# A two-layer hybrid trunk on one core: attention masks ahead of the scores, and one operand of each seven-product block summed by a second load

## The chip, the cores and the metric

The kernel runs on one core of one Trainium2 chip. The metric is device time in microseconds (us) of one execution. Engines are named as in the profile: PE does matrix products, PEld its weight loads, DVE is the vector engine, ACT the scalar engine, POOL the GpSimd engine, SP issues loads.

## What is computed

Two layers; in each, x passes through three sub-layers, every one between two RMSNorms and added back to x:

```
for l in range(DEPTH):                       # DEPTH 2, x is (1, 256, 1024) float32
    f = _swiglu(_rmsnorm(h, ff1_norm_pre[l]), ff1_w_gate[l], ff1_w_up[l], ff1_w_down[l])
    h = h + 0.5 * _rmsnorm(f, ff1_norm_post[l])
    m = _hybrid_mixer(_rmsnorm(h, mix_norm_pre[l]), w_in[l], ..., w_out[l])
    h = h + _rmsnorm(m, mix_norm_post[l])
    f = _swiglu(_rmsnorm(h, ff2_norm_pre[l]), ff2_w_gate[l], ff2_w_up[l], ff2_w_down[l])
    h = h + 0.5 * _rmsnorm(f, ff2_norm_post[l])

def _swiglu(h, wg, wu, wd):                  # 1024 -> 2816 -> 1024
    return (jax.nn.silu(h @ wg) * (h @ wu)) @ wd
```

The mixer puts three head groups side by side: a chunked state-space scan, a pooling group, and causal attention with four heads of 64 dimensions over the 256 tokens. Weights and results are float32.

## The kernel before

**Weights and precision.** Nearly all the work is weight matrices against 256 tokens. A weight comes in units of 128 x 2048 float32 (1 MB), loaded by SP (`load`, L77) into one of four `raw` buffers. Each unit, or a sum or difference of units, is a *job*: ACT writes `hi`, a copy rounded for the matrix engine (L102), DVE writes `lo = raw - hi` (L103), each in two pieces of 1024 columns. A job that is a sum first has DVE add two raw buffers (L101). A product of two split operands takes three passes: hi by hi, hi by lo, lo by hi. Up to five split jobs are held ahead of their use (`pump`, `get`, `done`).

**An FFN** has 2816 inner features in 11 blocks of 256. Blocks 0 and 1 are done token half by token half (`mm_half`, L317). Blocks 4, 7 and 10 are plain pairs of gate and up (`mm_feat`, L298). Blocks 2, 5 and 8, each with the one behind it, form a *quad*: a seven-product scheme in Strassen's manner (`ffn_quad`, with `product`, L428). The four quarters of a quad's weights are called g1, u1, g2 and u2, and its jobs are g1, u2, g2 and four sums: T1 = g1 + u1, T2 = T1 + u2, T3 = T2 - g1 (which is u1 + u2), T4 = T2 + g2. The left operands, S1 to S4 and parts X of the normalised tokens, are made at the start of each FFN (L281 to L287). Down projections (`mm_rows`, L334) of earlier blocks lie between the products of a quad. There are 3 quads in an FFN, 4 FFNs, so 12 quads.

In `plan_ffn` (L360 to L377) T1, T2 and T4 are built one upon the other in u1's raw buffer, T3 in g1's; g1's buffer is given back after T3, u1's after T4.

**Attention scores** (L676 to L686) are taken per row half: the two heads of a pair lie on rows 0 to 63 and 64 to 127. For each half and each pair a 128 x 128 block of scores (L683), its mask (a product of two bf16 constants that adds a large negative number, L684), a 128 x 256 block (L685) and a mask on its right half (L686) go one after another.

**Order.** The code is written once, and a scheduler puts each engine's instructions in an order of its own by their dependences; an engine then executes its own list strictly in that order, and waits where an operand isn't there. So a late operand holds up all that stands behind it on its engine.

Of the kernel before, what the change touches and what calls it, by code (L numbers as in the profile page):

```python
# [13 lines left out]
AF = mybir.ActivationFunctionType  # L14
ALU = mybir.AluOpType
AX = mybir.AxisListType

P = 128
# [29 lines left out]
class Weights:  # L48
# [9 lines left out]
        self.units.append((src, cols))  # L58
        return len(self.units) - 1

    def job(self, unit, sum_of=None, free=(), pieces=2):


        self.jobs.append((unit, sum_of, free, pieces))
        return len(self.jobs) - 1

    def plan(self, src, cols=UNIT, pieces=2):
# [18 lines left out]
    def split_next(self, only=None):  # L86

        i, nc = self.split, self.nc
        u, sum_of, free, pieces = self.jobs[i]
        cols, raw = self.units[u][1], self.raw[u]  # L90
        if i not in self.parts:
            self.parts[i] = [self.splitp.tile([P, KD * QDT], F32R, tag=x, name=f"{x}{i}") for x in ("hi", "lo")]
        hi, lo = self.parts[i]
        step = cols // pieces
        for c in range(0, cols, step):
            if only and c // step not in only:
                continue
            s = slice(c, c + step)
            if sum_of:
                x, op, y = sum_of  # L100
                nc.vector.tensor_tensor(raw[:, s], self.raw[x][:, s], self.raw[y][:, s], op=op)  # L101
            nc.scalar.activation(hi[:, s], raw[:, s], AF.Copy)  # L102
            nc.vector.tensor_tensor(lo[:, s], raw[:, s], hi[:, s].bitcast(F32), op=ALU.subtract)  # L103
        if only and pieces - 1 not in only:
            return
        for v in free:
            del self.raw[v]
            self.live -= 1
        self.split += 1
        self.held += 1  # L110
# [25 lines left out]
def hybrid_trunk_kernel(ctx: ExitStack, tc: tile.TileContext, a, out: bass.AP):  # L136
    nc = tc.nc
# [9 lines left out]
    def buf(dtype=F32, n=512, tag="t"):  # L147
        return tmp.tile([P, n], dtype, tag=tag, name=f"{tag}{next(ids)}", bufs={"t": 22, "n": 8}[tag])
# [4 lines left out]
    def bank(tag="wk"):  # L153
        return psum.tile([P, 512], F32, tag=tag, name=f"{tag}{next(ids)}")
# [4 lines left out]
    W = Weights(nc, rawp, splitp)  # L159
# [178 lines left out]
    def plan_ffn(l, n):  # L338


        p = {}

        def down(i):
            p["d", i] = W.plan(a[f"ff{n}_d"][l, i])

        def pair(i):
            for k in "gu":
                p[k, i] = W.plan(a[f"ff{n}_{k}"][l, PAIRS.index(i)])

        for i in range(2):  # L350
            for k in range(2):
                p["f", i, k] = W.plan(a[f"ff{n}_f"][l, 2 * i + k], pieces=4)
        before = list(FIRST)
        for i in range(2, NU):
            if i in PAIRS:
                pair(i)
                for b in before:
                    down(b)
                before = [i]
            elif i in QUADS:  # L360
                src = a[f"ff{n}_q"][l, QUADS.index(i)]
                g1, u1, u2 = (W.unit(src[k]) for k in (0, 1, 3))
                p["T1", i] = W.job(u1, (g1, ALU.add, u1))
                p["g1", i] = W.job(g1)
                p["T2", i] = W.job(u1, (u1, ALU.add, u2))
                p["T3", i] = W.job(g1, (u1, ALU.subtract, g1), free=(g1,))
                late = i == QUADS[-1]
                if not late:
                    down(before[0])
                g2 = W.unit(src[2])  # L370
                p["g2", i] = W.job(g2)
                for b in before[1:]:
                    down(b)
                p["T4", i] = W.job(u1, (u1, ALU.add, g2), free=(u1, g2))
                p["u2", i] = W.job(u2, free=(u2,))
                if late:
                    down(before[0])  # L377
                before = [i, i + 1]
        for b in before:
            down(b)  # L380
        return p
# [40 lines left out]
    def product(ps, left, job, first):  # L422

        hi, lo = (w[:, :UNIT].rearrange("p (k n) -> p k n", k=4) for w in W.get(job))
        parts = [(k, i) for i in range(3) for k in range(4)]
        for n, (k, i) in enumerate(parts):
            x, w = ((left[0], hi), (left[0], lo), (left[1], hi))[i]
            nc.tensor.matmul(ps, x[:, k, :], w[:, k, :], start=first and n == 0, stop=n == len(parts) - 1,  # L428
                             skip_group_check=not first)
        W.done(job)  # L430

    def ffn_quad(i, p, left, turn, downs):


        late = i == QUADS[-1]
        turn(0)
        pc = bank()
        product(pc, left["S1"], p["T1", i], True)
        h1 = buf()
        nc.scalar.activation(h1, pc, AF.Copy)  # L440
        pa = bank()
        product(pa, left["X11"], p["g1", i], True)
        w2 = buf()
        nc.scalar.activation(w2, pa, AF.Copy)
        turn(1)
        W.pump()
        pb = bank()
        product(pb, left["S2"], p["T2", i], True)
        nc.vector.tensor_tensor(w2, pb, w2, op=ALU.add)
        nc.vector.tensor_tensor(pc, pc, w2, op=ALU.subtract)  # L450
        W.pump()
        pd = bank()
        product(pd, left["S3"], p["T3", i], True)
        nc.vector.tensor_tensor(pd, pd, w2, op=ALU.add)
        nc.vector.tensor_tensor(h1, h1, pd, op=ALU.subtract)
        W.pump()
        if not late:
            downs[0]()
        product(pa, left["X12"], p["g2", i], False)
        h0 = buf()  # L460
        nc.scalar.activation(h0, pa, AF.Silu)
        W.pump()
        for f in downs[1:]:
            f()
        product(pd, left["X22"], p["T4", i], False)
        nc.scalar.activation(w2, pd, AF.Silu)
        nc.vector.tensor_tensor(h1, h1, w2, op=ALU.mult)
        W.pump()
        product(pc, left["S4"], p["u2", i], False)
        nc.vector.tensor_tensor(h0, pc, h0, op=ALU.mult)  # L470
        W.pump()
        if late:
            downs[0]()
        return [h0, h1]
# [74 lines left out]
    def mixer(l, p, turned, next_left, before_next):  # L549
# [125 lines left out]

        s0, s1 = banks2(), banks2()  # L676
        for j in range(2):
            r = slice(j * 64, (j + 1) * 64)
            for pr in range(2):
                q_ = qT[r, pr * 256 : (pr + 1) * 256]  # L680
                k_ = kT[r, pr * 256 : (pr + 1) * 256]
                o0, o1 = s0[j][:, pr * P : (pr + 1) * P], s1[j][:, pr * 256 : (pr + 1) * 256]
                nc.tensor.matmul(o0, q_[:, :P], k_[:, :P], start=True, stop=False)  # L683
                nc.tensor.matmul(o0, ident_b, neg_b, start=False, stop=True)  # L684
                nc.tensor.matmul(o1, q_[:, P:], k_, start=True, stop=False)  # L685
                nc.tensor.matmul(o1[:, P:], ident_b, neg_b, start=False, stop=True)  # L686

        def softmax(ps, n):

# [383 lines left out]
```

## Time and profile before

| | |
|---|---|
| runs | 963.24, 967.30, 967.02 us; median 967.02 |
| span of the profiled execution, the one time that it gives | 964.0 us |
| ACT busy | 583.2 us |
| L102, hi | 440 pieces, 399.6 us of ACT |
| L103, lo | 440 pieces, 466.4 us of DVE |
| read from memory | 176.07 MB |

The page gives the busy time of each engine, then groups of instructions: line, engine, operation, output and inputs, count, busy time and mean time of one, and how long the engine sat idle before them and for whom. A timeline row gives the start of an instruction or a run of like ones, its time, engine, line, tiles, count, and in square brackets the idle time before it with what ended it. A row of the view by stretches gives the time, the busy time and count of PE, PEld, DVE, ACT and POOL, the granted clock of the matrix engine (1.00 is full), the share of the DMA engines, and GB/s.

### The profile page before, as it was taken

What the parts mean: (1) busy time and instruction counts of PE and PEld (TensorE: products, weight loads), DVE (VectorE), ACT (ScalarE), POOL (GpSimd) and SP (SyncE); (2) the same over time, 40 slices, a digit from 0 to 9 for tenths busy, and PEclk for the clock granted to TensorE, in tenths of its full rate; (3) what the DMA queues carried; (4) which work ended last, traced back from release to release, by engine and by line L of the source; (5) the groups of instructions that cost most, each with busy time, mean ns of one, the idle gap of its engine ahead of it and who ended that gap; (6) DMA issues with size and microseconds to landing.
All of it is one profiled execution on the core that took longest, in us unless ns stands there. A gap on an engine that the chain in (4) does not pass through costs nothing.

```text
span 964.0 us, 13044 instructions
## 1 busy us (share of the span) xinstructions
PE 942.5 (98%) x5066; PEld 802.9 (83%) x5066; DVE 816.2 (85%) x1091; ACT 583.2 (61%) x923; POOL 21.8 (2%) x35
## 2 busy tenths in 40 slices
PE   7899999999999999999999999999999999999997
PEld 4689898888988779888977888888888877889896
DVE  6998899688787989889698989996878798989982
ACT  6655557477646565657466656666675565656651
POOL 0000000010001000000000000000000100000000
PEclk9989999998999999999999999999999999999999
DMA  8474456665243255455742737294733242827251
GB/s 327 151 266 171 177 216 241 242 209 184 89 159 119 90 201 237 169 225 215 265 174 85 276 112 294 88 343 161 270 121 131 88 154 88 330 99 301 85 190 44
DMA packets 26274, 177.96 MB, mean 185 GB/s; under 512 B 2914, under 2 KB 3170, under 8 KB 5732
## 3 DMA queue, kind: packets, MB, share of 16 engines
q1 hardware_dynamic: 26212, 177.13, 49.5%
q8 instruction: 40, 0.66, 0.3%
q14 instruction: 22, 0.18, 0.1%
HBM read 176.07 MB, written 1.05 MB: 184 GB/s over the span
## 4 chain that ended last, share of the span: by engine, by line
PE 74%; DVE 12%; ACT 8%; issue 3%; DMA 2%; POOL 1%; DVEq 0%; POOLq 0%; SPq 0%; ACTq 0%
PE acc L334 24%; PE wk L428 20%; PE wk L298 20%; DVE lo L103 5%; ACT hi L102 5%; PE wk L317 5%; DVE raw L101 2%; ACT n L223 2%; POOL s L217 1%; PE wk L403 1%; DVE n L207 1%; DMA raw<-in_ff_q 1%; DVE xT L207 1%; PE wk L863 1%; DVE n L249 1%
## 5 line engine op out<-in xcount | busy, mean ns | idle before, releaser
L102 ACT ACTIVATE hi<-raw 128x1024 fp32r<-128x1024 f32 (+2 forms) x440 | 399.6, 959 | 173.6 <-DVE raw L101 62.5
L103 DVE TENSOR_TENSOR lo<-raw,hi 128x1024 fp32r<-128x1024 f32 (+2 forms) x440 | 466.4, 1100 | 18.7 <-ACT hi L102 17.9
L334 PE MATMUL acc<-hi,t 128*128 128x512 f32 x832 | 221.9, 396 | 6.8 <-ACT hi L102 6.6
L334 PEld LDWEIGHTS acc<-hi,t 128*128 128x128 f32 x832 | 154.6, 189 | 42.1 <-ACT hi L102 9.1
L298 PE MATMUL wk<-xT,hi 128*128 128x256 f32 x1088 | 147.6, 288 | 0.0
L298 PEld LDWEIGHTS wk<-xT,hi 128*128 128x128 f32 x1088 | 140.1, 196 | 1.7
L334 PE MATMUL acc<-lo,t 128*128 128x512 f32 x416 | 116.0, 394 | 0.0
L101 DVE TENSOR_TENSOR raw<-raw,raw 128x1024 f32<-128x1024 f32 x96 | 113.8, 1216 | 2.0 <-DMA raw<-in_ff_q 2.0
L317 PE MATMUL wk<-hi,xT 128*128 128x512 f32 x384 | 101.3, 396 | 3.9 <-ACT xT L206 1.8
L428 PE MATMUL wk<-hi,n 128*128 128x512 f32 x384 | 101.8, 392 | 0.0
L334 PEld LDWEIGHTS acc<-lo,t 128*128 128x128 f32 x416 | 79.0, 190 | 16.9 <-DVE lo L103 0.2
L317 PEld LDWEIGHTS wk<-hi,xT 128*128 128x128 f32 x384 | 71.0, 188 | 21.7 <-ACT hi L102 3.1
L428 PEld LDWEIGHTS wk<-hi,n 128*128 128x128 f32 x384 | 71.6, 188 | 15.6 <-DVE wk L450 1.1
L298 PE MATMUL wk<-xT,lo 128*128 128x256 f32 x544 | 77.6, 285 | 0.0
L428 PE MATMUL wk<-hi,xT 128*128 128x512 f32 x288 | 77.2, 390 | 0.1
L298 PEld LDWEIGHTS wk<-xT,lo 128*128 128x128 f32 x544 | 71.1, 194 | 0.0
L428 PEld LDWEIGHTS wk<-hi,xT 128*128 128x128 f32 x288 | 53.6, 188 | 11.8 <-issue 0.5
L206 ACT ACTIVATE t<-wk 128x256 fp32r<-128x256 f32 x72 | 26.8, 377 | 55.4 <-PE wk L403 30.6
L317 PE MATMUL wk<-lo,xT 128*128 128x512 f32 x192 | 52.5, 393 | 1.1 <-DVE lo L103 1.0
L428 PE MATMUL wk<-lo,n 128*128 128x512 f32 x192 | 51.4, 390 | 0.0
L231 DVE TENSOR_TENSOR n<-acc,gains 128x512 f32<-128x512 f32 x24 | 16.5, 688 | 35.9 <-ACT n L223 35.9
L317 PEld LDWEIGHTS wk<-lo,xT 128*128 128x128 f32 x192 | 35.9, 188 | 10.0 <-DVE lo L103 2.3
(175 smaller groups left out, 764.6 us busy)
## 6 DMA issues: line engine op xcount, KB each, us to landing
raw<-in_ff_q SPq DMA_DIRECT2D x48, 1024.0 KB, 6.9
raw<-in_ff_d SPq DMA_DIRECT2D x44, 1024.0 KB, 6.5
raw<-in_ff_f SPq DMA_DIRECT2D x16, 1024.0 KB, 6.2
raw<-in_ff_g SPq DMA_DIRECT2D x12, 1024.0 KB, 5.8
raw<-in_ff_u SPq DMA_DIRECT2D x12, 1024.0 KB, 5.1
raw<-in_w_in SPq DMA_DIRECT2D x10, 1024.0 KB, 5.0
raw<-in_w_kvz SPq DMA_DIRECT2D x8, 1024.0 KB, 7.2
raw<-in_w_out SPq DMA_DIRECT2D x8, 1024.0 KB, 5.4
```

The source lines that it names most:

```text
L101: nc.vector.tensor_tensor(raw[:, s], self.raw[x][:, s], self.raw[y][:, s], op=op)
L102: nc.scalar.activation(hi[:, s], raw[:, s], AF.Copy)
L103: nc.vector.tensor_tensor(lo[:, s], raw[:, s], hi[:, s].bitcast(F32), op=ALU.subtract)
L206: split_into.last = nc.scalar.activation(hi, src_f32, AF.Copy)
L207: nc.vector.tensor_tensor(lo, src_f32, hi.bitcast(F32), op=ALU.subtract)
L217: nc.gpsimd.tensor_tensor(r, v, halfexp, op=ALU.pow)
L223: nc.scalar.activation(junk, x, AF.Square, scale=1.0 / (gain * math.sqrt(n)), accum_out=ssq)
L231: nc.vector.tensor_tensor(fg[i], f[i], gains[:, 1, i * 512 : (i + 1) * 512], op=ALU.mult)
L298: nc.tensor.matmul(ps, w[:, k, s], y[:, k, :], start=i == 0 and k == 0, stop=i == 2 and k == KD - 1)
L317: m = nc.tensor.matmul(ps, y[:, k, :], w[:, k, :], start=h == 0 and n == 0, stop=h == 1 and n == len(parts) - 1)
L334: nc.tensor.matmul(acc[b], x[:, j, s], w[:, j, b * 512 : (b + 1) * 512], start=first and j == 0 and i == 0, stop=last and j == 1 and i == 2)
L428: nc.tensor.matmul(ps, x[:, k, :], w[:, k, :], start=first and n == 0, stop=n == len(parts) - 1, skip_group_check=not first)
```

## The change

Two edits.

1. **Scores.** The eight mask products of a layer are done first, and the score products are then accumulated on top of them, with the row half as the innermost loop, so that neighbouring products lie on different row halves.
2. **Quads.** g1 is split first. T1, T2 and T4 are then built one upon the other in g1's raw buffer. As soon as T1's last add is done, POOL issues a second load of u2's 1 MB that adds to u1's raw buffer in place. T3 is then a plain job on that buffer, with no add on DVE, and u1's buffer is given back after T3. In `ffn_quad` g1's product moves ahead of T1's.

```
-    def job(self, unit, sum_of=None, free=(), pieces=2):
-        self.jobs.append((unit, sum_of, free, pieces))
+    def job(self, unit, sum_of=None, free=(), pieces=2, add=None):
+        self.jobs.append((unit, sum_of, free, pieces, add))
...
             if sum_of:
                 x, op, y = sum_of
                 nc.vector.tensor_tensor(raw[:, s], self.raw[x][:, s], self.raw[y][:, s], op=op)
+                if add and c + step == cols:
+                    nc.gpsimd.dma_start(self.raw[add[0]][:, :cols], add[1], accum_op=ALU.add)
...
-                p["T1", i] = W.job(u1, (g1, ALU.add, u1))
                 p["g1", i] = W.job(g1)
-                p["T2", i] = W.job(u1, (u1, ALU.add, u2))
-                p["T3", i] = W.job(g1, (u1, ALU.subtract, g1), free=(g1,))
+                p["T1", i] = W.job(g1, (g1, ALU.add, u1), add=(u1, src[3]))
+                p["T2", i] = W.job(g1, (g1, ALU.add, u2))
+                p["T3", i] = W.job(u1, free=(u1,))
...
-                p["T4", i] = W.job(u1, (u1, ALU.add, g2), free=(u1, g2))
+                p["T4", i] = W.job(g1, (g1, ALU.add, g2), free=(g1, g2))
...
         turn(0)
+        pa = bank()
+        product(pa, left["X11"], p["g1", i], True)
+        w2 = buf()
+        nc.scalar.activation(w2, pa, AF.Copy)
         pc = bank()
         product(pc, left["S1"], p["T1", i], True)
         h1 = buf()
         nc.scalar.activation(h1, pc, AF.Copy)
-        pa = bank()
-        product(pa, left["X11"], p["g1", i], True)
-        w2 = buf()
-        nc.scalar.activation(w2, pa, AF.Copy)
...
         for j in range(2):
-            r = slice(j * 64, (j + 1) * 64)
-            for pr in range(2):
-                q_ = qT[r, pr * 256 : (pr + 1) * 256]
-                k_ = kT[r, pr * 256 : (pr + 1) * 256]
-                o0, o1 = s0[j][:, pr * P : (pr + 1) * P], s1[j][:, pr * 256 : (pr + 1) * 256]
-                nc.tensor.matmul(o0, q_[:, :P], k_[:, :P], start=True, stop=False)
-                nc.tensor.matmul(o0, ident_b, neg_b, start=False, stop=True)
-                nc.tensor.matmul(o1, q_[:, P:], k_, start=True, stop=False)
-                nc.tensor.matmul(o1[:, P:], ident_b, neg_b, start=False, stop=True)
+            for ps, n, at in ((s0[j], P, 0), (s1[j], 2 * P, P)):
+                for pr in range(2):
+                    nc.tensor.matmul(ps[:, pr * n + at : pr * n + at + P], ident_b, neg_b, start=pr == 0, stop=False,
+                                     skip_group_check=True)
+        for pr in range(2):
+            for s, n, q0 in ((s0, P, 0), (s1, 2 * P, P)):
+                for j in range(2):
+                    r = slice(j * 64, (j + 1) * 64)
+                    nc.tensor.matmul(s[j][:, pr * n : (pr + 1) * n], qT[r, pr * 256 + q0 : pr * 256 + q0 + P],
+                                     kT[r, pr * 256 : pr * 256 + n], start=False, stop=True, skip_group_check=True)
```

The lines behind the new ones move down by two or three, so L102 and L103 become L104 and L105.

**ACT at the first quad of FFN2, layer 0.** In the rows before, raw_2878 is u1's buffer (T2 here), raw_2624 is g1's (T3 here) and raw_2902 the first down projection's.

```order
L102 ACTIVATE hi_3063<-raw_2878 128x1024
L206 ACTIVATE n_2994<-t_2981 128x512
L206 ACTIVATE n_2999<-t_2818 128x512
L206 ACTIVATE t_3089<-wk_3093 128x2x128
L102 ACTIVATE hi_3071<-raw_2624 128x1024
L102 ACTIVATE hi_3081<-raw_2902 128x1024
L102 ACTIVATE hi_3071<-raw_2624 128x1024
L102 ACTIVATE hi_3081<-raw_2902 128x1024
```

In the rows of the change, at the same place, raw_2621 is g1's buffer (T2 here), raw_2875 is u1's (T3, filled up by the accumulating load) and raw_2899 the first down projection's.

```order
L208 ACTIVATE n_2989<-t_2976 128x512
L208 ACTIVATE n_2994<-t_2815 128x512
L104 ACTIVATE hi_3061<-raw_2621 128x1024
L104 ACTIVATE hi_3069<-raw_2875 128x1024
L104 ACTIVATE hi_3061<-raw_2621 128x1024
L104 ACTIVATE hi_3069<-raw_2875 128x1024
L104 ACTIVATE hi_3077<-raw_2899 128x1024 x2
```

T3's halves were taken in turn with the down projection's; now they are taken in turn with T2's, and the down projection's stand behind both.

**DVE at the same place.** Before, with lo_3064 of T2, lo_3072 of T3 and lo_3082 of the first down projection:

```order
L103 TENSOR_TENSOR lo_3064<-raw_2878,hi_3063 128x1024
L101 TENSOR_TENSOR raw_2624<-raw_2878,raw_2624 128x1024 x2
L207 TENSOR_TENSOR t_3090<-wk_3093,t_3089 128x2x128
L103 TENSOR_TENSOR lo_3072<-raw_2624,hi_3071 128x1024
L103 TENSOR_TENSOR lo_3082<-raw_2902,hi_3081 128x1024
```

In the change, with lo_3062 of T2, lo_3070 of T3 and lo_3078 of the down projection:

```order
L101 TENSOR_TENSOR raw_2621<-raw_2621,raw_2887 128x1024
L389 TENSOR_TENSOR t_3050<-wk_2999,t_3048 128x512
L105 TENSOR_TENSOR lo_3062<-raw_2621,hi_3061 128x1024 x2
L105 TENSOR_TENSOR lo_3070<-raw_2875,hi_3069 128x1024 x2
L105 TENSOR_TENSOR lo_3078<-raw_2899,hi_3077 128x1024 x2
```

The subtraction of two pieces between T2's lo and T3's lo (L101, raw_2624) is gone.

**PE at the scores of layer 0.** Before, for the first half (acc_2159 and acc_2161 are result banks, b_88 and b_89 the mask's constants):

```order
L683 MATMUL acc_2159<-t_2067,t_2060 128x128
L684 LDWEIGHTS b_88
L684 MATMUL acc_2159<-b_89,b_88 128x128
L685 MATMUL acc_2161<-t_2067,t_2060 128x256
L686 LDWEIGHTS b_88
L686 MATMUL acc_2161<-b_89,b_88 128x128
```

In the change, behind eight masks in a row (acc_2156 and acc_2158 belong to the lower row half, acc_2157 and acc_2159 to the upper):

```order
L688 MATMUL acc_2156<-t_2064,t_2057 128x128
L688 MATMUL acc_2157<-t_2064,t_2057 128x128
L688 MATMUL acc_2158<-t_2064,t_2057 128x256
L688 MATMUL acc_2159<-t_2064,t_2057 128x256
L688 MATMUL acc_2156<-t_2064,t_2057 128x128
```

Neighbouring score products now lie on different row halves, and no mask stands between them. Each such row is two instructions in the trace, as a float32 product takes two passes.

More of the change, by code (lines that the diff above doesn't have):

```diff
@@ L88, in split_next @@
         i, nc = self.split, self.nc
-        u, sum_of, free, pieces = self.jobs[i]
+        u, sum_of, free, pieces, add = self.jobs[i]
         cols, raw = self.units[u][1], self.raw[u]
```

## The prediction

> **What bounds the kernel now.** I read the busy table of the page first, then what PE waited for, and only then stretches of the timeline.
>
> ```profile
> span 964.0 us, 13044 instructions
> PE 942.5 (98%) x5066; PEld 802.9 (83%) x5066; DVE 816.2 (85%) x1091; ACT 583.2 (61%) x923; POOL 21.8 (2%) x35
> PE acc L334 <- ACT hi L102: 6.6, 7, 2.4
> PE wk L317 <- ACT xT L206: 1.8, 5, 0.5
> ```
>
> PE is busy for 942.5 of 964.0 us. So the change can gain only in three ways: PE has less to do, PE waits less, or PE runs at a higher clock. The largest wait is L334 (the first down projection of each FFN) for ACT's hi, 6.6 us in 7 pieces. Half of it stands at the first FFN:
>
> ```profile
> 43.61 0.60 PE L403 MATMUL wk<-ident,t 128*128 128x128 f32 x4
> 46.57 1.24 PE L334 MATMUL acc<-hi,t 128*128 128x512 f32 x4 [2.36 <-ACT hi L102]
> 48.46 2.08 PE L334 MATMUL acc<-hi,t 128*128 128x512 f32 x4 [0.66 <-ACT hi L102]
> 50.34 2.76 PE L334 MATMUL acc<-lo,t 128*128 128x512 f32 x6
> 52.90 1.79 PE L334 MATMUL acc<-hi,t 128*128 128x512 f32 x4
> 54.53 1.08 PE L428 MATMUL wk<-hi,n 128*128 128x512 f32 x4
> 331.31 0.60 PE L403 MATMUL wk<-ident,t 128*128 128x128 f32 x4
> 331.67 1.18 PE L428 MATMUL wk<-hi,n 128*128 128x512 f32 x4
> 332.69 1.08 PE L428 MATMUL wk<-lo,n 128*128 128x512 f32 x4
> 333.61 1.08 PE L428 MATMUL wk<-hi,n 128*128 128x512 f32 x4
> ```
>
> Two waits, 2.36 + 0.66 = 3.0 us. Behind them 14 matmuls take from 48.46 to 54.53, 6.07 us, where four take 0.92 us at 332.69 (332.69 to 333.61), so 3.2 for 14: another 2.9 us is lost. The clock explains it, and it drops at two other places, after the attention scores of each layer:
>
> ```profile
> 44.00:56.00 12.00, 8.98 (x27) 6.62 (x26) 11.09 (x15) 8.06 (x12) 0.00 (x0) 0.72 0.46 175
> 234.00:246.00 12.00, 12.00 (x50) 9.56 (x50) 8.38 (x19) 5.04 (x15) 0.00 (x0) 0.57 0.01 1
> 708.00:714.00 6.00, 6.00 (x34) 5.42 (x34) 5.15 (x16) 3.50 (x11) 0.00 (x0) 0.72 0.00 0
> ```
>
> The column ahead of the DMA share is the granted clock. With PE busy throughout, 12 us at 0.57 lose 5.2 us and 6 us at 0.72 lose 1.7.
>
> **The quad jobs: what is taken out.** Each of 12 quads loses T3's subtraction, 2 adds on DVE:
>
> ```profile
> L101 DVE TENSOR_TENSOR raw<-raw,raw 128x1024 f32<-128x1024 f32 x96 | 113.8, 1216 | 2.0 <-DMA raw<-in_ff_q 2.0
> 316.00:340.00 24.00, 22.20 (x104) 17.56 (x102) 24.00 (x29) 14.74 (x20) 0.00 (x0) 1.00 0.21 66
> ```
>
> That is 24 x 1.216 = 29.2 us of DVE. Taken as a whole it is worth nothing, because DVE is busy 85% of the time and PE does not wait for it in the middle of an FFN. It counts where DVE is full: at the start of each FFN, as between 316 and 340 (24.00 of 24.00), when PE at the end of that stretch waits for what stands behind the subtraction:
>
> ```profile
> 316.15 2.35 DVE L101 TENSOR_TENSOR raw<-raw,raw 128x1024 f32<-128x1024 f32 x2
> 324.90 1.21 DVE L101 TENSOR_TENSOR raw<-raw,raw 128x1024 f32<-128x1024 f32 x1
> 334.79 2.35 DVE L101 TENSOR_TENSOR raw<-raw,raw 128x1024 f32<-128x1024 f32 x2
> 336.03 3.90 ACT L102 ACTIVATE hi<-raw 128x1024 fp32r<-128x1024 f32 x4 [3.70 <-DVE raw L101]
> 338.09 0.73 PE L334 MATMUL acc<-hi,t 128*128 128x512 f32 x2 [0.25 <-ACT hi L102]
> 339.99 0.73 PE L334 MATMUL acc<-hi,t 128*128 128x512 f32 x2 [1.16 <-ACT hi L102]
> ```
>
> This is FFN2 of layer 0. ACT stands idle for 3.70 us until T3's subtraction (334.79) gives it a first half, and its four hi from 336.03 are T3's and the down's in turn. In the changed order ACT does T2, T3, T2, T3, down, down in one go. I put T3's first turn at 330.4, from DVE's and ACT's rows one after another (T2's adds end at 326.1, two normalising steps lie between). Six hi of 0.98 us (3.90 / 4) then begin at 329.4 and end at 335.3, where PE reaches the down at 337.6. So the waits of 0.25 and 1.16 go, if the data of T3 is there.
>
> **The accumulating DMA: what is put in.** T3's operand is now made by a 1 MB transfer that POOL issues once T1's second add is done. The trace has no DMA from POOL, and none that adds. Call L the time from that add to landing. The nearest rows:
>
> ```profile
> raw<-in_ff_q SPq DMA_DIRECT2D x48, 1024.0 KB, 6.9
> L217 POOL TENSOR_TENSOR s<-s,halfexp x28: 547/681/1394, 6.1 to 959.1; 128x1 f32<-128x1 f32 x28
> 26.26 2.35 DVE L101 TENSOR_TENSOR raw<-raw,raw 128x1024 f32<-128x1024 f32 x2
> ```
>
> The same source and size lands in 6.9 us from SP; POOL's one operation takes 0.55 us at best and 1.39 at worst. Low end: 6.9. High end: 6.9 stretched as POOL's worst row is, x 2.55, 17.6. I take L = 8, the load and one or two POOL steps, since the load is the nearest row. From the Trainium skill ("DMA: Bandwidth & Descriptors", section "Anatomy of one DMA — SWDGE (gpsimd) path"), which gives about 2.0 us plus bytes / 436e3 for a DMA issued by GpSimd, 1 MB would be an estimated 4.4 us; the sum would then be 1.7 us better at the first FFN and the same elsewhere. No run here shows that yet.
>
> What is queued behind it: on POOL only L217's powers of later norms. On ACT, behind T3's first half, T2's second half and both halves of the first down. So down's first hi ends about 4 hi, 4 us, after the landing.
> - FFN2, layer 0: T1's adds ended at 318.5; g1's lo now goes ahead, so 319.8. Down's hi is there at 323.8 + L; PE needs it at 337.6. No wait up to L = 13.8. I take the same margin for FFN1 and FFN2 of layer 1. Gain: the part of the 6.6 us that is not at the first FFN, 6.6 - 3.0 = **3.6 us**.
> - FFN1, layer 0 is tighter. T1's adds ended at 28.6 (26.26 + 2.35). Now two of g1's lo, one of T1's and four normalising steps go ahead of the second one: some 33.65. Down's hi ends at 37.65 + L; PE is free at 43.97 (43.61 and four transposes at 0.09, as at 331.31). With L = 8 PE waits 1.7 us instead of 3.0 and, as I choose, keeps its clock, which saves 1.3 + 2.9 = **4.2 us**. With L = 6.9 it would be 5.3; with L = 10 the wait is 3.7 and the clock drops as before, a loss of 0.7.
> - Later quads have more room:
>
> ```profile
> 373.16 2.36 DVE L101 TENSOR_TENSOR raw<-raw,raw 128x1024 f32<-128x1024 f32 x2 [0.51 <-DMA raw<-in_ff_q]
> 396.92 1.07 PE L428 MATMUL wk<-lo,n 128*128 128x512 f32 x4
> ```
>
> T1's adds end at 375.5 and T3's product begins some 20 us later: room to L = 17 or so with T3's hi and lo in between. Cost: nothing. The 12.6 MB more on 178 MB stand against a DMA share of 49.5% and cost nothing while the loads run ahead.
>
> g1's product now goes before T1's; the same matmuls, no cost.
>
> **The scores.** PE does the same 24 matmul instructions a layer (16 of the scores, 8 masks) in another order. Before (the first six rows layer 1, the next two layer 0, the last two a later stage of layer 0):
>
> ```profile
> 704.03 0.49 PE L683 MATMUL acc<-t,t 64*128 64x128 f32 x2
> 704.45 0.23 PE L684 MATMUL acc<-b,b 128*128 128x128 bf16 x1
> 704.61 0.70 PE L685 MATMUL acc<-t,t 64*128 64x256 f32 x2
> 705.24 0.23 PE L686 MATMUL acc<-b,b 128*128 128x128 bf16 x1
> 705.40 0.49 PE L683 MATMUL acc<-t,t 64*128 64x128 f32 x2
> 709.34 0.23 PE L686 MATMUL acc<-b,b 128*128 128x128 bf16 x1
> 232.12 0.49 PE L683 MATMUL acc<-t,t 64*128 64x128 f32 x2
> 235.48 1.22 PE L685 MATMUL acc<-t,t 64*128 64x256 f32 x2
> 267.04 0.32 PE L818 MATMUL acc<-t,t 128*64 128x128 f32 x1
> 267.05 0.43 PE L816 MATMUL acc<-t,t 128*64 128x256 f32 x1
> ```
>
> By the start-to-start times one step is 0.42 + 0.16 + 0.63 + 0.16 = 1.37 us; four are 5.4. The masks in a row: 8 x 0.09 (the transposes' pace) to 8 x 0.16; I take 0.7. The scores cost 4 x 1.05 = 4.2 in sequence. Alternating row halves may run side by side; the rows at 267.04 and 267.05 show two matmuls on different column halves starting 10 ns apart, and no row shows row halves. Ends: 2.1 (pairs fully beside each other) and 4.2 (not at all). I take 2.7. Stage: 3.4 instead of 5.4, so **1.9 us** a layer after rounding, 3.8 in all. The Trainium skill ("TensorE: Matmul & The Clock Gate", "Part 3: Packing small matmuls — row/col tiling") says that matmuls on different row groups run concurrently, 3.07 times faster with four. By that rule the pairs would reach 2.1 and the sum would be 1.2 us better.
>
> The clock: the drops follow a long run of half-height fp32 matmuls. In layer 0 the scores begin at 232.12, and at 235.48 the pair that takes 0.70 us at full clock already takes 1.22: 3.4 us of half-height work went before. In layer 1 they keep their pace to the end (709.34), and the clock is down in the stretch around it. A stage of 3.4 us, with both halves of the array in use, leaves hardly a stretch of that length with nothing but half-height work. I take both drops as gone: 5.2 + 1.7 = **6.9 us**; the other end is 0.
>
> **Sum.** 3.6 + 4.2 + 3.8 + 6.9 = 18.5 us. The profiled span, 964.0, becomes 945.5. The span lies 3.0 us under the median of the runs shown (967.02; 963.24 to 967.30), so against that median I say 948.5, rounded to 948.
>
> **Rivals.**
> 1. *The row halves don't run side by side.* For it: each fp32 score matmul loads weights for 64 rows, and spacing at 704.03 leaves those loads visible. Against it: the 10 ns at 267.04. Only the masks gain, 0.6 us a layer, and both drops of the clock stay. 964.0 - 7.8 - 1.2 = 955, reported 958.
> 2. *The accumulating DMA lands late: slower.* Place: T3's hi on ACT at the four FFN starts, with T2's second half and down behind it. At L = 17.6 down's hi at the first FFN ends at 55.3, where it was there at 46.5: 8.7 lost and the old drop of the clock kept. At the other three it ends 17.6 - 13.8 = 3.8 late, where 3.6 in all were lost before: 11.4 - 3.6 = 7.8, and PE, idle for 4 us in each, would lose 2.9 more to the clock as at 48.46: 8.7. Together 25 lost, against 10.7 from the scores: 964.0 + 14.5 = 978, reported 981. It decides from L of about 15. For it: DVE is full at those four places, and POOL's row ranges up to 1.39. Against it: POOL's row is 0.68 in the middle. The Trainium skill ("SBUF — State Buffer", section "SBUF: two separate sides") speaks for this rival: it says that DMAs issued from GpSimd starve for descriptors while DVE holds the shared port, 620 ns becoming about 3100 in its example. Whether DVE's adds and subtractions do that here, no row shows, since nothing is issued from POOL.
> 3. *Nothing moves.* L is 10 to 14, so the first FFN loses about what the others gain, and the clock drops after the scores come at another moment only. Then only 3.8 or less of the scores stays: 960 to 964, reported 963 to 967.
>
> **Chances.** Forecast 0.52, rival 1 0.20, rival 2 0.14, rival 3 0.14. A measurement of this kernel can tell about 0.5% from no change, 4.8 us. Faster by more than that: the forecast and rival 1, and a little of rival 3, 0.73. Slower: rival 2, 0.13. Within: 0.14. The range: the best ends together (5.3 at the first FFN, 2.1 for the pairs, and the waits of L317 going in part) give 6 us more than 18.5, 942; a luckier clock could take some more, so 938 below. Above, it takes in rivals 1 and 3: 968. Rival 2's 981 is left out.
>
> **What would show it.** Right: PE's wait at L334 falls from 6.6 to about 2; the first down starts at 45.7; score matmuls of both halves start within tens of ns and the stage lasts 3.4 us; the clock stays 1.00 behind it; POOL's transfers land about 8 us after the second add. Wrong: ACT's hi waits for a DMA of POOL's queue with PE waiting behind it, and clock windows of 0.5 at the FFN starts; or score matmuls that follow each other at 0.21 and 0.31 us as before.

## The result and the profile after

The change takes 950.28 us (median of 4 runs, 949.99 to 950.96), the kernel before 966.25 (median of 4, 963.24 to 967.30). The ratio is 0.9841, with a 95% interval from 0.9823 to 0.986. The forecast was 948.

First the head of the page of the change, its waits of PE, and the row of the new loads among the DMA issues.

```profile
span 949.3 us, 13147 instructions
PE 929.7 (98%) x5066; PEld 794.9 (84%) x5066; DVE 789.8 (83%) x1067; ACT 580.5 (61%) x923; POOL 34.7 (4%) x47
PE acc L336 <- ACT hi L104: 2.9, 1, 2.9
PE acc L336 <- DVE lo L105: 1.5, 3, 0.5
PE acc L714 <- ACT t L702: 1.6, 2, 0.8
raw<-in_ff_q SPq DMA_DIRECT2D x48, 1024.0 KB, 5.0
raw<-in_ff_q POOLq DMA_DIRECT2D x12, 1024.0 KB, 8.0
```

PE is still busy 98% of the span. Its 6.6 us of waits for the first down projections became 2.9 in one piece, at the first FFN, and three pieces of 0.5 us at the others. A new wait of 0.8 us stands in each mixer. DVE lost 26 us of work. The accumulating loads land in 8.0 us, where SP's loads of the same size take 5.0 in the same execution.

To see where the time went, I took the same PE rows in both traces as milestones (the transposes ahead of a down projection, the turning of the normalised tokens, and so on) and compared the lengths between them:

```
change minus before, us      after   scores  masks   quads  sum on  load in  load
                             change  only    first   only   DVE     halves   late
start, to 43.61               1.71   -0.46    0.39    0.43  -0.53   -0.44    1.28
first quad of FFN1, layer 0  -1.47   -1.83   -1.85   -0.19  -3.57   -4.99    2.18
mixer, layer 0               -6.71   -6.73   -6.86   -2.90  -6.68   -6.67   -6.79
first quad of FFN2, layer 0  -1.56    0.81    0.16   -1.57  -1.01   -1.54    4.12
first quad of FFN1, layer 1  -1.21    0.21    0.00   -1.22  -0.67   -1.21    3.62
mixer, layer 1               -3.83   -3.80   -3.94    1.40  -3.50   -3.83   -3.79
first quad of FFN2, layer 1  -1.25    1.58    0.34   -1.27  -0.73   -1.26    4.58
all the rest                 -0.51   -0.30   -0.23   -0.44  -1.03   -0.47   34.93
sum, to 938.25              -14.83  -10.52  -11.99   -5.76 -17.72  -20.41   40.13
```

Each column is one profiled execution. The other columns are the experiments below. In the change, the two mixers give 10.5 us, the three later FFN starts 4.0, the first one 1.5, and the start of the kernel takes back 1.7.

The timeline of the first FFN in the change, PE, then ACT, DVE and POOL; the last two rows are ACT's and PE's at FFN2 of layer 0:

```profile
45.32 0.60 PE L405 MATMUL wk<-ident,t 128*128 128x128 f32 x4
48.86 3.80 PE L336 MATMUL acc<-hi,t 128*128 128x512 f32 x8 [2.94 <-ACT hi L104]
41.52 1.06 ACT L104 ACTIVATE hi<-raw 128x1024 fp32r<-128x1024 f32 x1 [1.10 <-DVE raw L101]
44.91 4.84 ACT L104 ACTIVATE hi<-raw 128x1024 fp32r<-128x1024 f32 x5 [2.32 <-DMA raw<-in_ff_q]
34.88 1.22 DVE L101 TENSOR_TENSOR raw<-raw,raw 128x1024 f32<-128x1024 f32 x1
36.73 1.04 POOL L103 DMA_DIRECT2D raw<-in_ff_q  x1 [20.16 <-ACT n L208]
324.48 5.81 ACT L104 ACTIVATE hi<-raw 128x1024 fp32r<-128x1024 f32 x6 [2.63 <-DVE raw L101]
330.83 1.17 PE L336 MATMUL acc<-hi,t 128*128 128x512 f32 x4
```

T1's second add ends at 36.1, the load is issued at 36.73 and landed at 44.9, 8.8 us after the add. ACT has done T2's first half by 42.6 and waits 2.32 us for the landing with five hi behind it, and PE waits 2.94 for the down's hi. At FFN2 ACT does its six hi without a gap, held back only by T2's add, and PE finds the down's hi.

The scores of layer 0, and stretches of the three places where the clock had dropped:

```profile
232.13 0.62 PE L682 MATMUL acc<-b,b 128*128 128x128 bf16 x8
232.68 1.58 PE L688 MATMUL acc<-t,t 64*128 64x128 f32 x16
234.19 1.33 PE L300 MATMUL wk<-xT,hi 128*128 128x256 f32 x9
236.31 0.39 PE L714 MATMUL acc<-dA,cst 128*128 128x8 f32 x2 [0.78 <-ACT t L702]
44.00:56.00 12.00, 9.06 (x35) 6.83 (x34) 8.49 (x12) 8.28 (x12) 0.00 (x0) 0.86 0.46 170
230.00:246.00 16.00, 15.22 (x125) 14.01 (x124) 14.22 (x31) 14.24 (x44) 0.00 (x0) 1.00 0.33 126
700.00:714.00 14.00, 14.00 (x108) 13.41 (x108) 10.73 (x22) 12.24 (x25) 0.00 (x0) 1.00 0.23 76
```

Masks 0.55 us, scores 1.51: a stage of 2.06 us. The granted clock behind it is 1.00 in both layers. At the first FFN it is 0.86 instead of 0.72: 12 us at 0.86 hold 3.4 us at half clock, where 12 at 0.72 held 6.7.

### The profile page after: what moved, and what is told of

Its sections match the earlier page's. It is cut to its first block, busy times and chain, and to the rows that moved or that the text cites. A ratio compares the mean times of both kernels' runs of the same rounds, so it can differ in the third digit from the quotient of the medians.

```text
span 949.3 us, 13147 instructions
## 1 busy us (share of the span) xinstructions
PE 929.7 (98%) x5066; PEld 794.9 (84%) x5066; DVE 789.8 (83%) x1067; ACT 580.5 (61%) x923; POOL 34.7 (4%) x47
## 3 DMA queue, kind: packets, MB, share of 16 engines
HBM read 188.65 MB, written 1.05 MB: 200 GB/s over the span
## 4 chain that ended last, share of the span: by engine, by line
PE 71%; DVE 11%; ACT 7%; issue 4%; POOL 1%; DMA 1%; POOLq 0%; DVEq 0%; ACTq 0%
PE acc L336 25%; PE wk L430 22%; PE wk L300 18%; DVE lo L105 5%; ACT hi L104 2%; PE wk L319 2%; ACT n L225 2%; POOL s L219 1%; DVE raw L101 1%; PE wk L405 1%; ACT n L669 1%; DMA raw<-in_ff_q 1%; DVE xT L209 1%; DVE n L209 1%; PE wk L866 1%
## 5 line engine op out<-in xcount | busy, mean ns | idle before, releaser
L105 DVE TENSOR_TENSOR lo<-raw,hi 128x1024 fp32r<-128x1024 f32 (+2 forms) x440 | 468.1, 1102 | 62.5 <-ACT hi L104 61.9
L104 ACT ACTIVATE hi<-raw 128x1024 fp32r<-128x1024 f32 (+2 forms) x440 | 399.4, 959 | 176.9 <-PE wk L300 37.5
L300 PE MATMUL wk<-xT,hi 128*128 128x256 f32 x1088 | 144.0, 285 | 0.0
L300 PEld LDWEIGHTS wk<-xT,hi 128*128 128x128 f32 x1088 | 136.8, 192 | 2.3 <-issue 0.7
L101 DVE TENSOR_TENSOR raw<-raw,raw 128x1024 f32<-128x1024 f32 x72 | 86.3, 1217 | 1.7 <-DMA raw<-in_ff_q 1.6
L319 PEld LDWEIGHTS wk<-lo,xT 128*128 128x128 f32 x192 | 36.1, 189 | 9.8 <-DVE lo L105 2.2
```

Of the source, the lines that this page charges most:

```text
L300: nc.tensor.matmul(ps, w[:, k, s], y[:, k, :], start=i == 0 and k == 0, stop=i == 2 and k == KD - 1)
L319: m = nc.tensor.matmul(ps, y[:, k, :], w[:, k, :], start=h == 0 and n == 0, stop=h == 1 and n == len(parts) - 1)
```

## Experiments

### One edit at a time, and the scores taken apart

The first four kernels: the scores' edit alone; the masks first with the scores in the old order; the alternation with the masks in between; the quads' edit alone.

> Only the scores edit is made (masks first, row halves alternating); the quads stay as before. Theory: the two mixers gave 10.4 us of the 14.7 by which the profiled span fell (6.65 in layer 0, 3.74 in layer 1), and they need nothing of the quads. Expected 966.3 - 10.4 = 956 us, the stage at about 2.1 us, the granted clock 1.00 behind it. Rival: the low clock comes and goes by the moment at which its windows fall, so that with the old FFN starts it falls after the scores again; then only the shorter stage is left, 3.3 us a layer, 959 to 960 us.

Measured: 955.34 us, ratio 0.9889 (0.9868 to 0.991). The mixers gain 6.73 and 3.80 us, as in the whole change, so this edit needs nothing of the other. (It loses 0.8 and 1.6 us at two FFN starts, where PE waits for DVE; I did not follow that up.)

The next kernel puts all masks first, as in the change, and then the scores half by half:

```
+        for j in range(2):
+            for pr in range(2):
+                for s, n, q0 in ((s0, P, 0), (s1, 2 * P, P)):
+                    r = slice(j * 64, (j + 1) * 64)
+                    nc.tensor.matmul(s[j][...], qT[r, ...], kT[r, ...], start=False, stop=True, ...)
```

> Masks first as in the change, but the scores in the old order, one row half after the other; the quads stay as before. Theory (row halves run side by side, masks cost little): the eight masks fall from 1.28 to 0.55 us a layer, the scores stay at 4.2, the stage at 4.8; half-height work still fills a window, so the low clock behind the scores stays: 964 to 965 us. Rival (each mask between two scores is what cost the time, by a change of type or by draining the array): the stage falls to about 2.1 us here too and the low clock goes: 956 us.

Measured: 953.65 us, ratio 0.9882 (0.9861 to 0.9902). My theory fell: without alternation in the order the mixers gain as much, 6.86 and 3.94 us. PE's timeline and the clock; the last two rows are what runs on PE in two stretches of 0.15 us, 232.05 to 232.20 and 232.95 to 233.10:

```profile
230.55 0.62 PE L680 MATMUL acc<-b,b 128*128 128x128 bf16 x8
231.10 2.34 PE L686 MATMUL acc<-t,t 64*128 64x128 f32 x16
233.37 2.18 PE L298 MATMUL wk<-xT,hi 128*128 128x256 f32 x16
235.70 0.39 PE L712 MATMUL acc<-dA,cst 128*128 128x8 f32 x2
230.00:246.00 16.00, 15.97 (x124) 14.68 (x124) 14.44 (x30) 14.26 (x41) 0.00 (x0) 1.00 0.31 118
231.86 0.71 PE L686 MATMUL acc<-t,t 64*128 64x128 f32 x6
232.73 0.71 PE L686 MATMUL acc<-t,t 64*128 64x128 f32 x3
```

The scores take 2.27 us (231.10 to 233.37), not the 4.2 that they took with masks between. Moving the masks does not do all of that. The first two scores take 0.76 us (231.10 to 231.86), but the next four take 0.76 together (231.86 to 232.62) and the last two 0.75. So in the middle, where one row half gives way to the other, the halves run side by side: six products are on PE in a stretch of 0.15 us there, three in the later one. Four times 0.76, 3.0 us, would be the price in sequence.

The stage, 2.82 us, is 0.76 longer than in the change, but here PE does not wait for ACT at the product that follows (no bracket at 235.70): 17 products stand between the scores and it, where the change has 9 (the row at 234.19). So the mixer gains as much.

Then the alternation without masks first, two masks behind each pair:

```
+                for j in range(2):
+                    nc.tensor.matmul(s[j][...], qT[r, ...], kT[r, ...], start=True, stop=False)
+                for j in range(2):
+                    nc.tensor.matmul(s[j][...], ident_b, neg_b, start=False, stop=True)
```

> Row halves alternate, but each pair of scores is followed by its two masks, as near to the old place as that allows; the quads stay as before. Theory: each pair runs side by side, so the scores take about 1.5 to 2.1 us, the masks up to 1.3: a stage of 2.8 to 3.4 us, the low clock gone: 957 us. Rival (a mask on the whole array keeps the pairs apart): the stage stays above 4 us and the low clock too, 963 us or more.

Measured: 954.28 us, ratio 0.9887 (0.9867 to 0.9906). Its timeline:

```profile
229.91 0.49 PE L681 MATMUL acc<-t,t 64*128 64x128 f32 x4
230.33 0.28 PE L684 MATMUL acc<-b,b 128*128 128x128 bf16 x2
230.55 0.70 PE L681 MATMUL acc<-t,t 64*128 64x256 f32 x4
231.18 0.28 PE L684 MATMUL acc<-b,b 128*128 128x128 bf16 x2
```

A pair takes 0.42 and 0.63 us, just what one score took before: twice the work in the same time. The stage is 2.85 us, and the mixers gain 6.69 and 3.83. So either half of the edit alone gives all of its gain, the masks first with the help of the one place where the halves meet.

> Only the quads' edit is made; the scores stay as before. Theory: the four FFN starts gave 1.5 + 1.6 + 1.2 + 1.3 = 5.5 us in the profile; expected 966.3 - 5.5 = 961 us, 959 to 963 since low clocks at the starts and after the scores can fall otherwise. PE's wait at the down projection for ACT's hi is 2.9 us in one piece. Rival: the quads give nothing of their own and the starts gained only by a luckier clock: 964 to 966 us.

Measured: 959.28 us (955.19 to 960.03), ratio 0.9927 (0.9901 to 0.9953). The three later starts gain 1.57, 1.22 and 1.27, as in the change. The first one gains 0.19, which is nothing. The clock still drops behind the old scores, in these stretches of layers 0 and 1:

```profile
236.00:246.00 10.00, 10.00 (x63) 9.20 (x63) 7.59 (x18) 5.00 (x15) 0.00 (x0) 0.83 0.08 12
700.00:710.00 10.00, 10.00 (x46) 8.00 (x46) 7.58 (x19) 5.04 (x15) 0.00 (x0) 0.66 0.00 0
```

With PE busy throughout, 10 us at 0.83 lose 1.7 us in layer 0 and 10 at 0.66 lose 3.4 in layer 1; the kernel before lost 5.2 and 1.7. How long a drop lasts varies; in both profiles of a kernel with the long stage it comes in both layers. One of the four runs here, at 955.19 us, shows a mean granted clock of 0.995 where the others show 0.987 to 0.989; it has no trace, so how its drops fell is not known.

### What made a lone score slow

```
-                nc.tensor.matmul(o0, ident_b, neg_b, start=False, stop=True)
+                nc.tensor.matmul(o0, ident_b[r, :], neg_b[r, :], start=False, stop=True)
```

(and the same for o1), everything else as before. This kernel leaves out half of the mask.

> The kernel before with its order of scores and masks, but each mask product covers only the 64 rows of its score's half, so half of the mask is left out of the result. It tells what about the mask made a lone score slow: before, a score's two instructions followed each other at 0.21 and 0.31 us, with masks out of the way at about 0.11 and 0.18. Theory: the change between 64 and 128 rows in the array costs it; with the mask on 64 rows too, the pace is 0.11 to 0.18, the stage about 3.2 us, the low clock behind it gone: 954 to 956 us. Rival: the change of type between float32 and bf16, or the mask's own weight load, costs it: the pace stays at 0.21 and 0.31, the stage at 5.4, 962 to 966 us.

Measured: 955.9 us (two runs), ratio 0.9902 (0.9863 to 0.9941). PE's timeline at the first scores of layer 0; the last two rows are weight loads (PEld) of a mask, here and in the kernel before:

```profile
230.59 0.48 PE L683 MATMUL acc<-t,t 64*128 64x128 f32 x2
230.91 0.22 PE L684 MATMUL acc<-b,b 64*128 64x128 bf16 x1
230.97 0.65 PE L685 MATMUL acc<-t,t 64*128 64x256 f32 x2
231.46 0.22 PE L686 MATMUL acc<-b,b 64*128 64x128 bf16 x1
231.79 0.22 PE L684 MATMUL acc<-b,b 64*128 64x128 bf16 x1
231.79 0.37 PE L683 MATMUL acc<-t,t 64*128 64x128 f32 x1
233.68 1.33 PE L298 MATMUL wk<-xT,hi 128*128 128x256 f32 x9
231.24 0.09 PEld L686 LDWEIGHTS <-b 64*128 64x128 bf16 x1
705.24 0.10 PEld L686 LDWEIGHTS <-b 128*128 128x128 bf16 x1 [0.33 <-issue]
```

With the same order and the same alternation of types, but no change of height, a score of 128 columns takes 0.32 us instead of 0.42 and one of 256 takes 0.49 instead of 0.63; a mask takes 0.06 instead of 0.16. The stage is 3.09 us instead of 5.35, and the clock keeps 1.00 behind it. Type is excluded as the main cost. The load rows show one place where the time went: before, the mask's weights are loaded only when its own product starts (both at 705.24), here 0.22 us earlier, while the score still runs (231.24, product at 231.46). The load itself takes 0.09 to 0.10 us in both, so its size is not the cost. At 231.79 the mask of the one row half and the score of the other start together, so part of this, too, is halves side by side: four steps of 0.93 us (0.32 + 0.06 + 0.49 + 0.06) would be 3.7 us.

### The accumulating load

```
-                p["T3", i] = W.job(u1, free=(u1,))
+                p["T3", i] = W.job(u1, (u1, ALU.add, u2), free=(u1,))
```

and T1's job without the load.

> The whole change, but u1 + u2 is made by two adds on DVE (T3 as a sum job) and not by the accumulating load; the order of the jobs and products stays the changed one. Theory: the three later FFN starts gain about 1.3 us each because DVE, full there, has 2.4 us less to do; with the adds back they lose that: 950.3 + 4 = 954 us, and the first FFN, which gained nothing by the quads, keeps its wait of 3 us. Rival: it is the order (g1 first, its lo split ahead of the norm) that gained: 950 us.

Measured: 948.49 us (948.30 to 950.23), ratio 0.9829 (0.9801 to 0.9857). The theory was wrong on the whole: without the load the kernel is no slower. The later starts gain 1.01, 0.67 and 0.73 us, 2.4 of the change's 4.0, and the first one gains 3.57 instead of 1.47. DVE and ACT at FFN2 of layer 0, then PE at the first FFN:

```profile
307.34 2.36 DVE L101 TENSOR_TENSOR raw<-raw,raw 128x1024 f32<-128x1024 f32 x2
311.41 1.22 DVE L101 TENSOR_TENSOR raw<-raw,raw 128x1024 f32<-128x1024 f32 x1
313.74 1.22 DVE L101 TENSOR_TENSOR raw<-raw,raw 128x1024 f32<-128x1024 f32 x1
322.01 5.80 ACT L104 ACTIVATE hi<-raw 128x1024 fp32r<-128x1024 f32 x6 [0.81 <-DVE raw L101]
43.08 0.60 PE L405 MATMUL wk<-ident,t 128*128 128x128 f32 x4
43.61 0.73 PE L336 MATMUL acc<-hi,t 128*128 128x512 f32 x2
44.56 1.63 PE L336 MATMUL acc<-hi,t 128*128 128x512 f32 x6 [0.21 <-ACT hi L104]
```

The adds at 311.41 and 313.74 are T3's. As u1 + u2 it needs neither T2 nor g1's lo, so they run right behind T1's (307.34), long before T2's, and ACT does its six hi in one go here too. The order with g1 first is kept in this kernel, so how much of the 2.4 us is that order, the rival expected here, was not taken apart. At the first FFN PE reaches the down at 43.6 and finds its hi.

> The whole change, but the accumulating load is issued after T2's last add instead of T1's, so that it lands later by what lies between: 42.6 - 36.1 = 6.5 us at the first FFN, 326.1 - 314.0 = 12 us at FFN2 of layer 0. It tells whether a late landing costs what the prediction's second rival said (down's first hi four hi behind the landing, ACT and PE waiting). Theory: the landing at FFN2 is at 326.1 + 8.4 = 334.5, down's first hi at 338.5 instead of 329.3, PE needs it at 330.8: 7 to 8 us lost at three starts, 6.5 at the first, and 1 to 2 us of low clock at some of them: 950 + 30 = 980 us (975 to 986). If PE finds other work, or the later quads have no room, it would be 955 to 965 or over 990.

Measured: 949.67 us, ratio 0.9839 (0.981 to 0.9869), and no answer. The load moved in the program but not in time: POOL issued it at 313.89, where the change has 314.45, since it waits for nothing of T2's.

```profile
313.89 0.91 POOL L103 DMA_DIRECT2D raw<-in_ff_q  x1 [5.22 <-DMA gains<-in_gains]
```

So it counts as one more run of the change. The next kernel makes the load wait in truth.

```
+                    first = self.raw[add[0]][:, :1]
+                    nc.vector.scalar_tensor_tensor(first, raw[:, cols - 1 : cols], 0.0, first, op0=ALU.mult, op1=ALU.add)
                     nc.gpsimd.dma_start(self.raw[add[0]][:, :cols], add[1], accum_op=ALU.add)
```

> As in the run before it with the load at T2, but now the load really waits: DVE adds nothing (0 times a column of T2) to one column of u1's buffer once T2's last add is done, and the accumulating load waits for that. The result stays the same. Theory (the prediction's second rival as a mechanism): the load is issued some 7.5 us later at the first FFN and some 13 us later at the other three starts, T3's hi waits for it with the first down's hi behind it on ACT, and PE waits: 7 to 8 us at each start more than in the change, and 1.7 to 3.4 us of low clock behind some of the waits: 980 to 990 us, slower than the kernel before. If a late landing is harmless, 950.

Measured: 1006.54 us, ratio 1.0426 (1.0386 to 1.0467). POOL's row at FFN2 of layer 0, the greatest wait of PE, and the stretch behind:

```profile
338.55 0.92 POOL L105 DMA_DIRECT2D raw<-in_ff_q  x1 [19.12 <-DVE raw L104]
PE wk L432 <- ACT hi L106: 16.8, 6, 5.5
343.00:355.00 12.00, 8.23 (x25) 6.00 (x24) 6.93 (x9) 3.90 (x4) 0.00 (x0) 0.72 0.54 159
```

The transfer itself is no slower (landing 7.9 us after issue, the median of 12), but PE is busy for only 8.23 of 12 us there and its clock falls. I expected 980 to 990 us. The four starts lose 14.5 us against before, less than the 25 of the second rival, though the loads landed 17 us after T1's add at the first FFN (35.7 to 52.6) and 22 at FFN2 of layer 0 (324.3 to 346.7). PE now waits mostly at a product of the quad (L432) and not at the down projection. The later quads lose most: 34.9 us in all the rest. So a late landing is dear, as the second rival said, but not mainly at the place that it named.

### Two remedies for the first FFN

```
-                if add and c + step == cols:
-                    nc.gpsimd.dma_start(self.raw[add[0]][:, :cols], add[1], accum_op=ALU.add)
+                if add:
+                    nc.gpsimd.dma_start(self.raw[add[0]][:, s], add[1][:, s], accum_op=ALU.add)
```

> The whole change, but the accumulating load is issued in two halves, each as soon as T1's add of that half is done (at the first FFN 30.8 and 36.1). Theory: at the first FFN the wait of ACT for the landing (2.3 us, 42.6 to 44.9) sets PE's wait of 2.94; with the first half landed by 40 and the second by 43, down's hi comes 2 us earlier, and the low clock of 1.7 us behind it may go: 947 to 948.5 us. Rival: half a load takes nearly as long as a whole one, and two issues take twice POOL's time, so nothing is won: 950.

Measured: 946.34 us, ratio 0.9803 (0.9774 to 0.9831). POOL's and PE's rows:

```profile
29.27 1.03 POOL L103 DMA_DIRECT2D raw<-in_ff_q  x1 [13.78 <-DVE t L283]
34.23 0.88 POOL L103 DMA_DIRECT2D raw<-in_ff_q  x1 [3.93 <-DVE raw L101]
44.26 0.73 PE L336 MATMUL acc<-hi,t 128*128 128x512 f32 x2 [0.49 <-ACT hi L104]
43.00:55.00 12.00, 11.30 (x50) 8.56 (x49) 10.52 (x13) 8.04 (x13) 0.00 (x0) 1.00 0.47 175
```

PE's wait falls from 2.94 to 0.7 us in two pieces, and the clock stays up. The first quad gains 4.99 us over before, 3.5 more than in the change.

> The whole change, but in the first quad of an FFN the down projection's job stands ahead of T3's, so that on ACT and DVE nothing that PE needs first stands behind the landing. Theory: at the first FFN PE's wait of 2.94 us and the low clock behind it (3.4 us at half, 1.7 lost) go, the 0.5 us waits for lo at the other three starts too: 950.3 - 2.9 - 1.7 - 1 = 945 us, 944 to 948. Rival: the wait moves to T3's product, which PE needs some 6 us later: 948 to 950.

Measured: 946.60 us, ratio 0.9805 (0.9768 to 0.9841). No wait for ACT's hi at the first down is left, and the first quad gains 5.84 us. At the other three starts I expected 1 us more and got nothing: the waits for lo give way to three of up to 0.6 us for another operand that DVE makes, t. So it was the place behind the landing that cost the time at the first FFN, whichever way it is taken away.

> The same kernel as the one with the load in two halves, beside the change on one chip: 946 to 947 us, 3 to 4 us under the change, since at the first FFN PE no longer waits and no low clock follows. If the first time was luck of the clock's windows, 949 to 950.

> The change itself, beside the kernel with the load in two halves: 950 us, with a wait of about 3 us at the first down projection and 1.7 to 3.4 us lost to low clock behind it.

Measured side by side: 945.89 us (945.67 to 947.36) and 950.38 us (949.33 to 951.10); ratios to before 0.9803 (0.9777 to 0.9828) and 0.9844 (0.9819 to 0.9869). The kernel with the load in halves beats both, the change by 4.5 us. In the two profiles 3.7 us of the difference lie in the first quad (-5.00 against -1.34), and 1.4 at the start (-0.09 against 1.32).

## Why the prediction was right, and where its steps were not

The forecast of 948 us lies 2.3 us under the measured 950.28, and the way was right. In the span the miss is larger, 945.5 forecast and 949.3 measured: 18.5 us were forecast and 14.7 came. The forecast then added 3.0 us between span and median, which were 1.0 here; that the two came so close is partly luck. Its terms, in the profiles:

- **Score stage and clock together: 10.7 forecast, 10.5 measured.** The clock was right: no drop is left behind a short stage, in any profile of a kernel that has one. The stage was mis-sized, 3.4 us forecast and 2.06 measured, and the reason was wrong. I took 4.2 us as the price of the scores in sequence and the alternation as the only lever. An estimate from the runs: two scores, one of each width, take 0.76 us when no mask stands between them, and 1.05 between full-height masks, so each such stretch costs some 0.14 us more. Two alternating pairs take the same 0.76 (the change, 232.68 to 233.44) and 1.05 (masks between), so the halves run fully side by side. Four steps of these are 4.2 before, 2.1 with alternation alone and 1.5 in the change. Both levers are there, and either is enough. The stage's extra gain did not reach the end: PE now waits 0.78 us at L714 for ACT. Over both layers the stage gives 6.6 us (5.35 to 2.06 twice) and the waits take 1.6; what is left for the clock is some 5.5 of the 6.9 forecast. So an under-sized gain, an unseen wait and an over-sized price of the clock cancelled in the sum, which is luck.
- The Trainium skill ("TensorE: Matmul & The Clock Gate", "Part 3: Packing small matmuls — row/col tiling") says that matmuls on different row groups run concurrently. The runs agree: four scores in alternating pairs take the 0.76 us that two take in sequence.
- **The three later FFN starts: 3.6 forecast, 4.0 measured** (1.56 + 1.21 + 1.25). The place was right: six hi in one go on ACT (324.48), down's hi in time. The cause was right only in part. With the two adds still on DVE, 2.4 of the 4.0 remain. So 1.6 us come from the adds being off DVE. The larger part comes with T3 no longer hanging on T2, which the trace shows, and with g1 split first; the runs do not part these two.
- **The first FFN: 4.2 forecast, 1.5 measured, and none of it by the quads' edit.** Kernels with the old quads gain 1.83 and 1.85 there by a shorter drop of the clock or none, and the quads' edit alone, with a drop as long as before, gains 0.19. So the 1.5 us go with one period of half clock less, 3.4 us instead of 6.8. The step that failed is L, and with it the clock. I put T1's second add at 33.65 and L at 8. Measured are 36.1, of which 1.7 is the later start, so 34.4, and 8.8. Down's hi is then 1.6 us later in all than I said, PE waits 2.94 us instead of 1.7, about as long as before, and the clock drops again. The prediction's own bound came near it: with L = 10 nothing was left. Its sign of being wrong showed at this one place: ACT's hi waits for POOL's load, with PE behind it and half clock. The 2.9 us that it put down to the clock there were too much, too: with the masks first alone no drop is left there, and the same 14 products still take 4.2 us at full clock, with a wait of 0.40 us for lo among them, not the 3.2 that the forecast took.
- **The start, not forecast: 1.7 lost.** It is complete before PE's first product of a quad. The other profile of the change shows 1.3 there, the other kernels between 0.5 gained and 1.7 lost. The first load of weights landed some 0.6 us later and one period of half clock fell there; whether the change has a part in that stays open. In the run with the load moved behind T2, which is the change in effect, no such period falls there and 0.7 us are lost.
- **Rival 2** did not come about, but it was the right thing to fear. Over 12 loads the time from issue to landing lies between 7.8 and 9.1 us, with DVE 83% busy. Its price was put at the wrong place: where the load really came late, the four starts lost 14.5 us and not 25, but the later quads 34.9, since the room that I saw there was gone when the load waited for T2. The rule of the Trainium skill that was taken to speak for this rival ("SBUF — State Buffer", "SBUF: two separate sides": five times as long beside DVE) has a copy on DVE as its example, and says further on that tensor_tensor, the operation of DVE's adds and subtractions here, did not stall such a DMA. These runs agree with that. The skill's figure for a DMA from GpSimd ("DMA: Bandwidth & Descriptors", "Anatomy of one DMA — SWDGE (gpsimd) path", an estimated 4.4 us for 1 MB) was too low against the 8.0 measured. These runs don't tell whether the adding, POOL's issue or the other loads make that difference.

Open: why a drop of the clock at the first FFN lasts for one or two of its periods, or none, at nearly the same wait of PE. With waits of 2.4 to 3.2 us for hi, the traces show 3.4 and 6.8 us of half clock, and once none. Open too is what in the long score stage brings the drop. "Nothing but half-height work" does not fit as it stands, since full-height masks lay between the scores; the longest stage of half-height products alone that was run, 3.09 us (the half masks), brought none. Whether it is the length of the stage or the pauses between its products, these runs do not tell.

## What to carry to other kernels

When a derived operand is late, ask first what it is derived from: rewriting T3 from T2 - g1 to u1 + u2 freed it from a chain, and that, with g1 split first, was worth more than moving its adds to a DMA. A transfer that feeds an engine's strict queue should be issued in the pieces in which it is consumed, or stand behind what the bottleneck needs sooner. Matrix products that use half of the rows belong together, away from full-height ones; a gain there ends where the next engine's chain begins to bind.

## What was not expected of the hardware

- A half-height float32 score between full-height products costs about 0.14 us more per such stretch, by the estimate above, on 0.38 for the score itself.
- In all traces the half-clock periods within the work last 3.4, 6.8 or 10.2 us, that is one, two or three times 3.41 (12 us at 0.86, 0.72 and 0.57 in the stretches above hold 3.4, 6.7 and 10.3). One more such period at the start, or one fewer at the first FFN, moves this kernel by up to 1.7 us with no change in its code.
